# adaLN vectors as groups of 32-partition matmuls, scale1 in column blocks, one more ring slot, another order of pieces

## Chip, cores and metric

One core of a Trainium2 chip runs the whole layer. The metric is device time in microseconds of one execution; lower is better. Engines: PE (matmuls), DVE (vector engine), ACT (scalar engine), POOL (GpSimd), SP (the queue that issues most transfers).

## What is computed

One decoder layer on 256 tokens of width 1024, batch 1, all in float32:

```python
mod = silu(c) @ w_ada + b_ada                       # w_ada: 1024 x 6144
shift1, scale1, gate1, shift2, scale2, gate2 = split(mod, 6)
hn   = rms_norm(x, g_norm1) * (1 + scale1) + shift1
proj = hn @ w_in                                    # 1024 x 3592
q_m, k_m, v_m, o_m, gates, q_a, k_a, v_a = split(proj)
h_m  = rms_norm(mlstm(silu(conv(q_m, k_m)), v_m, gates)) * sigmoid(o_m)   # 4 heads x 128
h_a  = causal_attention(q_a, k_a, v_a)              # 8 heads x 64; one block of 256 keys
x    = x + gate1 * (concat(h_m, h_a) @ w_out)
hn2  = rms_norm(x, g_norm2) * (1 + scale2) + shift2
# router: top 1 of 4 groups, top 2 of its 8 experts; 32 SwiGLU experts, 1024 -> 512 -> 1024
x    = x + gate2 * sum_of_chosen_experts(hn2)
out  = rms_norm(x, g_final)
```

The weights are 246 MB, of which 201 MB belong to the 32 experts. All of them are read.

## The kernel before

**Ring.** All large tiles are slots of 8.3 KB per partition in one pool of 18 (`RING`): a slot takes one block of 1 MiB of weights, or a large intermediate (x1, xnT, the two halves of h, q/k of attention, and so on). Loads are issued on SP in program order; a load waits until a slot is free, and what stands behind it on SP waits too. After the mixer's 43 blocks (24 of w_ada, 14 of w_in, 4 of w_out, x in two halves) come 192 blocks of experts, six for each.

**Before the steps.** x is normalised (L260 to 263) and transposed into `xnT`. scale1 is summed over 1024 rows: three row blocks by full-width matmuls with `silu(c)` repeated over 128 columns (L252), the other five by DVE (`ada_kc`, L211), and both sums are turned into columns by 16 matmuls of one column each (L285). Then `h_scaled` (L373) forms h without shift1 as a high and a low half.

**The 72 steps.** `steps` (L300) holds seven chunks of 512 columns of w_in with eight steps of 128 rows each (`ga` with the gate columns, `ka`, `va`, `qm`, `km`, `vm`, `om`), then 16 steps of w_out. In each step a weight block is split into `hi`, rounded to fp32r, and `lo`, the rest (`split`, L322, three steps ahead); `hi` is a cast on ACT or on DVE (`ON_DVE_H`, 31 of 72), `lo` a subtraction on POOL or on DVE (`ON_DVE_L`, 24 of 72). `step` (L339) makes three products (high by high, high by low, low by high) on PE. The first two chunks use h without shift1; `shift_rows` and `shift_bias` (L386, L394) compute shift1 @ w on DVE and add it as a bias (`evac_k`, `bias_q`). From `va` on, `h_full` (L400) has put shift1 into h.

**Pieces.** Everything else (conv, attention, mLSTM, adaLN sums, loads, transposes) is a list of named pieces (`op`, L722). `PLAN` (L43) gives the step ahead of which each is put. PE runs in exactly this order; for the other engines the framework orders the instructions within the dependencies. An adaLN section is summed row block by row block with a multiply-add over 1024 columns on DVE (`ada_kc`), four of them scaled on ACT and added on POOL (`ON_POOL_A`); then `ada_cols` (L222) makes columns with one-column matmuls, or `ada_bcast` (L230) and `gate2_rows` (L712) a row repeated over all partitions.

**After the steps.** Residual, second norm, router logits, choice of experts, and the first gather `pair(0)` (L897 to 985). Then 32 experts one after another: `gate_up` (L1003) and `down` (L1019) are matmuls of 32 columns of weights that write groups of 32 PSUM partitions.

Of the kernel before, what the change touches and what calls it, by code (L numbers as in the profile page):

```python
# [19 lines left out]
P = 128  # L20
D = 1024
# [14 lines left out]
RING = 18  # L36
# [27 lines left out]
ON_DVE_H = {0, 1, 3, 4, 5, 7, 11, 15, 16, 22, 24, 28, 29, 30, 31, 32, 36, 37, 39, 40, 42, 44, 45, 48, 49, 51, 52, 58, 60, 68, 70}  # L64
ON_POOL_A = {(2, 1), (2, 3), (2, 7), (5, 6)}
# [3 lines left out]
def tile_hymba_layer(  # L69
# [63 lines left out]
    A.dma_start(pk[0:8, :], rows(g_norm2))
# [70 lines left out]
    AW, ACC = {}, {}  # L204

    def ada_row(sec):
        acc = ACC[sec] = gate2 if sec == 5 else wk.tile([P, D], F32, name=f"acc{sec}", tag="acc")
        G.memset(acc, 0.0)
        G.dma_start(acc[0:1, :], b_ada[0:1, sec * D:(sec + 1) * D])

    def ada_kc(sec, kc):  # L211
        w = AW[sec, kc // 2][:, kc % 2, :]
        if (sec, kc) in ON_POOL_A:
            A.activation(w, w, AF.Copy, scale=csil[:, kc:kc + 1])
            G.tensor_tensor(ACC[sec], ACC[sec], w, op=ALU.add)
        elif sec not in ACC:
# [5 lines left out]
    def ada_cols(sec, permuted):  # L222
        acc = ACC[sec]
        p = bank(f"pc{sec}", (P, KC))
        a = acc.rearrange("q (p j) -> q j p", j=KC) if permuted else acc.rearrange("q (j p) -> q j p", j=KC)
# [4 lines left out]
    def ada_bcast(acc, dst, name):  # L230
        for h in range(2):
            p = bank(f"{name}{h}")
            T.matmul(p, ones, acc[:, h * 512:(h + 1) * 512], start=True, stop=True)
            A.activation(dst[:, h * 512:(h + 1) * 512], p, AF.Copy)

    csb = wk.tile([P, KC // 2, P], F32, name="csb", tag="k2")
    V.tensor_copy(csb, csil.rearrange("p (q k) -> p q k", k=2)[:, :, 0:1].to_broadcast([P, KC // 2, P]))

    def load_x():
        for tb in range(NT):  # L240
            nc.sync.dma_start(x1[:, tb, :], x2[:, tb, :])

# [1 line left out]
    pr = [bank(f"pr{h}", tag="pj") for h in range(2)]  # L244
    row = gate2[0:1, :]
    for q in range(4):
        load_ada(1, q)
        if q == 1:
            load_x()
        if q < 3:  # L250
            for h in range(2):
                T.matmul(pr[h], csb[:, q, :], AW[1, q][:, 0, h * 512:(h + 1) * 512], start=(q == 0), stop=(q == 2))  # L252
        else:
            ada_kc(1, 2 * q)
        ada_kc(1, 2 * q + 1)
        if q == 2:
            A.activation(row[:, 0:512], pr[0][0:1, :], AF.Copy)
            A.activation(row[:, 512:1024], pr[1][0:1, :], AF.Copy)
# [23 lines left out]
    p1 = bank("pc1", (P, KC))  # L282
    for part, k in ((row, 1), (ACC[1], P)):
        for j in range(KC):
            T.matmul(p1[:, j:j + 1], part[:, j * P:(j + 1) * P], ones[0:k, 0:1], start=(k == 1 and j == 0),  # L285
                     stop=(k == P), skip_group_check=True)
    s1 = const([P, KC], "s1")
    V.tensor_tensor(s1, p1, bsc1, op=ALU.add)
    V.scalar_tensor_tensor(s1, s1, 1.0, g1c, op0=ALU.add, op1=ALU.mult)

# [1 line left out]
    # the first two chunks use h without shift1 and get shift1 @ w as a bias  # L292
# [29 lines left out]
    def split(s):  # L322
# [8 lines left out]
        (V if s in ON_DVE_L else G).tensor_tensor(lo, src, hi.bitcast(F32), op=ALU.subtract)  # L331
# [967 lines left out]
```

## Time and profile before

| | us |
|---|---|
| median of 3 runs | 692.18 |
| lowest, highest | 692.13, 694.0 |
| span of the profiled execution | 690.9 |
| first projection matmul starts | 30.32 |
| last matmul of the output projection starts | 210.42 |
| first expert matmul starts | 226.74 |

The span runs from the first to the last instruction of one profiled execution; the median is 1.3 us above it. Over the whole span PE is busy 546.9 us (79%), DVE 286.1 (41%), ACT 128.5 (19%), POOL 116.7 (17%), and 248.80 MB are moved at a mean of 360 GB/s. These shares are means over stages that differ: read the 40 slices first (busy tenths of each engine, the transfers' share, GB/s), then the table by stage, then single lines of the timeline.

### The profile page before, as it was taken

The numbers are of one execution on the slowest core, as the hardware profiler recorded it, in microseconds if no ns is written. First come the engines' busy times: TensorE is split into PE (matmuls) and PEld (weight loads), VectorE is DVE, ScalarE is ACT, GpSimd is POOL, SyncE is SP. The second block draws the span as 40 slices with busy tenths as digits, with TensorE's granted clock in tenths as the row PEclk, the third lists the DMA queues.
The fourth block names the chain that finished last, engine by engine and source line by source line (L and its number), as shares of the span: only waits on it lengthen the run. The fifth ranks groups of instructions, "written<-read, shape, count | busy, mean of one in ns | idle before, by whom it ended". The sixth has DMA issues, their size and how long they took to land. (4 is left out here: it accounts for less than half of the span.)

```text
span 690.9 us, 15508 instructions
## 1 busy us (share of the span) xinstructions
PE 546.9 (79%) x6817; PEld 405.4 (59%) x6817; DVE 286.1 (41%) x609; ACT 128.5 (19%) x286; POOL 116.7 (17%) x109
## 2 busy tenths in 40 slices
PE   3998899699899898777777767686896877787575
PEld 1798688587687775663544545374564645454353
DVE  2699999999976432212212122122212122131212
ACT  2525445358325100000000000000000000000023
POOL 4265377646630100000000000000000000000000
PEclk9698889999879999979987988977788698698788
DMA  8999926558877899999999999999999999999992
GB/s 283 397 393 372 331 67 244 182 184 313 296 305 247 355 411 415 413 420 415 416 414 419 413 416 417 415 416 416 415 415 415 416 417 416 415 414 417 413 362 105
DMA packets 52864, 248.80 MB, mean 360 GB/s; under 512 B 4229, under 2 KB 4377, under 8 KB 36409
## 3 DMA queue, kind: packets, MB, share of 16 engines
q1 hardware_dynamic: 52256, 247.52, 90.2%
q8 instruction: 55, 0.90, 0.5%
q0 software_dynamic: 368, 0.20, 0.3%
q14 instruction: 17, 0.13, 0.0%
q10 hardware_dynamic: 168, 0.06, 0.0%
HBM read 246.70 MB, written 1.05 MB: 359 GB/s over the span
## 5 line engine op out<-in xcount | busy, mean ns | idle before, releaser
L1005 PE MATMUL pgu<-we,xg 128*32 128x128 f32 x4096 | 153.1, 302 | 56.1 <-DMA we<-in_w_expert_gate_dram 26.9
L1005 PEld LDWEIGHTS pgu<-we,xg 128*32 128x32 f32 x4096 | 124.9, 122 | 95.2 <-issue 36.7
L1021 PE MATMUL py<-wd,ht 128*32 128x256 f32 x992 | 78.6, 452 | 31.1 <-DVE ht L1016 15.6
L1012 DVE TENSOR_TENSOR hm<-sg,pgu 128x128 f32<-128x128 f32 x32 | 9.2, 288 | 220.4 <-ACT sg L1010 220.4
L1026 DVE TENSOR_TENSOR y<-py,gate 32x256 f32<-32x256 f32 x124 | 52.1, 420 | 92.3 <-PE py L1021 90.9
L1010 ACT ACTIVATE sg<-pgu 128x128 f32<-128x128 f32 x32 | 8.9, 277 | 392.5 <-PE pgu L1005 388.4
L882 PEld LDWEIGHTS pgx<-oh,xn 128*128 128x128 f32 x512 | 66.4, 211 | 6.0 <-issue 6.0
L882 PE MATMUL pgx<-oh,xn 128*128 128x64 f32 x512 | 69.9, 298 | 0.0
L1021 PEld LDWEIGHTS py<-wd,ht 128*32 128x32 f32 x992 | 31.3, 123 | 63.9 <-DVE ht L1016 22.6
L220 DVE SCALAR_TENSOR_TENSOR acc<-wa,csil,acc 128x1024 f32<-128x1024 f32 x30 | 49.4, 1647 | 4.9 <-DMA wa<-in_w_ada_dram 4.5
L872 POOL TENSOR_TENSOR ow<-oh,gg 128x128 f32<-128x128 f32 x16 | 5.9, 399 | 217.5 <-PE pw L1032 183.3
L825 PE MATMUL acc<-y,owt 128*128 128x512 f32 x64 | 34.6, 667 | 1.9 <-DVE y L1026 1.9
L1195 POOL MEMSET owz<- 128x1024 f32 x1 | 1.0, 951 | 201.5 <-PE pgu L1005 201.5
L1014 PE MATMUL ph<-ident,hm 128*128 128x128 f32 x32 | 10.8, 338 | 17.0 <-DVE hm L1012 17.0
L331 POOL TENSOR_TENSOR wl<-wo,wh 128x512 fp32r<-128x512 f32 x12 | 22.2, 1866 | 10.8 <-ACT wh L330 8.5
L886 DVE TENSOR_TENSOR xg<-pgx,s 128x256 f32<-128x256 f32 x32 | 12.2, 420 | 28.1 <-PE pgx L882 27.2
L825 PEld LDWEIGHTS acc<-y,owt 128*128 128x128 f32 x64 | 11.8, 206 | 15.0 <-issue 11.4
L1014 PEld LDWEIGHTS ph<-ident,hm 128*128 128x128 f32 x32 | 5.2, 161 | 24.5 <-DVE hm L1012 24.5
L337 PE MATMUL po<-wh,hTL 128*128 128x512 f32 x32 | 13.9, 433 | 4.4 <-DVE hTL L632 4.3
L252 PE MATMUL pr<-wa,csb 128*128 128x512 f32 x12 | 9.3, 917 | 8.5 <-DMA wa<-in_w_ada_dram 8.5
L335 PE MATMUL po<-wh,hTH 128*128 128x512 f32 x32 | 14.5, 452 | 0.0
L1016 DVE COPY ht<-ph 128x128 f32<-128x128 f32 x32 | 9.2, 289 | 10.4 <-PE ph L1014 10.4
(371 smaller groups left out, 883.1 us busy)
## 6 DMA issues: line engine op xcount, KB each, us to landing
we<-in_w_expert_gate_dram SPq DMA_DIRECT2D x64, 1024.0 KB, 20.0
we<-in_w_expert_up_dram SPq DMA_DIRECT2D x64, 1024.0 KB, 20.0
wd<-in_w_expert_down_dram SPq DMA_DIRECT2D x63, 1024.0 KB, 20.3
wa<-in_w_ada_dram SPq DMA_DIRECT2D x24, 1024.0 KB, 8.2
wo<-in_w_out_dram SPq DMA_DIRECT2D x4, 1024.0 KB, 5.0
wi_ga<-in_w_in_dram SPq DMA_DIRECT2D x2, 1040.0 KB, 11.2
wi_ka<-in_w_in_dram SPq DMA_DIRECT2D x2, 1024.0 KB
wi_qm<-in_w_in_dram SPq DMA_DIRECT2D x2, 1024.0 KB, 18.3
```

The lines of the kernel that those rows point to most:

```text
L220: V.scalar_tensor_tensor(ACC[sec], w, csil[:, kc:kc + 1], ACC[sec], op0=ALU.mult, op1=ALU.add)
L252: T.matmul(pr[h], csb[:, q, :], AW[1, q][:, 0, h * 512:(h + 1) * 512], start=(q == 0), stop=(q == 2))
L331: (V if s in ON_DVE_L else G).tensor_tensor(lo, src, hi.bitcast(F32), op=ALU.subtract)
L335: T.matmul(p, aH, bH, start=first, stop=False)
L337: T.matmul(p, aL, bH, start=False, stop=last)
L825: T.matmul(acc2[tb, h][:, cols], lhsT, rhs, start=start, stop=stop, skip_group_check=True)
L882: T.matmul(pj[j], xn2[:, tb, j, :], oh(tb), start=(tb == 0), stop=(tb == NT - 1))
L886: V.tensor_tensor(xg[:, js], src, s2[:, js].unsqueeze(2).to_broadcast([P, 4, n]), op=ALU.mult)
L1005: T.matmul(pgu[32 * g:32 * g + 32, u * P:(u + 1) * P], xg[:, j, :], wt[:, g * P:(g + 1) * P], start=j == 0 and u == 0, stop=j == KC - 1, s ...
L1014: T.transpose(ph, hm, ident)
L1021: T.matmul(py[32 * g:32 * g + 32, :], ht[:, 32 * f:32 * f + 32], wt[:, g * S:(g + 1) * S], start=first, stop=last, skip_group_check=True)
L1026: V.tensor_tensor(y4[r0:r0 + 32, g * S:(g + 1) * S], py[32 * g:32 * g + 32, :], gate2[r0:r0 + 32, g * S:(g + 1) * S], op=ALU.mult)
```

## The change

- `RING` goes from 18 to 19 slots; the DMA scratch of POOL's software queue is set to 4096.
- An adaLN section is summed in one PSUM tile of 128 x 256: partitions 32g to 32g+31 hold column part g (`ada_mm`, four matmuls of 32 weight columns for each source). Eight row blocks (shift1, gate1) or six of eight (scale2, shift2, gate2) are still multiply-adds on DVE (`ada_dve`, `ON_DVE_A`), whose sum enters as one more source; POOL does none.
- Columns come out of this tile with a masked product and a reduction (`own_column`, mask `m32`) in place of one-column matmuls; gate rows with `ada_rows` and two matmuls for each half (`ada_bcast`).
- scale1 is loaded as four blocks of 1024 rows x 256 columns (`load_scale1`) and formed in four parts before steps 0, 2, 4 and 6 (`scale1`).
- shift1 @ w for the first two chunks moves from DVE to such matmuls (`shift_bias`); the gate projection becomes eight matmuls of 256 columns and two small ones (`gate_rows8`, `gate_proj`).
- x is the first large load; the small vectors are split between ACT's and POOL's queues; xn is scaled on DVE.
- All `hi` casts are on ACT; `lo` is on POOL in 30 of 72 steps and otherwise on DVE; the first operation of `h_full` moves from ACT to DVE.
- `LOADS` and `PLAN` are rewritten; the transposes of x1's first half stand between the two halves of the last step.

```diff
-RING = 18
+RING = 19
 LOADS = """
-    ga0 ga1 ka0 ka1 A00 A01 A02 A03 qm0 va0 qm1 km0 va1 om0 vm0 km1 A20 vm1 A21 A40 A22 om1 W2 A23 A41 W1 A30 A42 W0
-    W3 A43 A31 A32 A50 A51 A33 A52 A53
+    ga0 B1 B2 ga1 B3 ka0 ka1 A00 A01 A02 A03 va0 va1 qm0 A20 qm1 A21 A22 A23 km0 km1 vm0 vm1 A40 om0 A41 om1 A42 A43 W2 W3
+    A30 A31 W0 A32 W1 A33 A50 A51 A52 A53
 PLAN
...
-    ldA33:41 ldA50:40 ldA51:41 ldA52:41 ldA53:41 gw0:5 gw1:6 sh0:-3 sh1:-3 sh2:-3 sh3:0 sh4:0 sh5:0 sh6:0 sh7:1
+    scl:24 hs0:-2 hs1:-2 sb1:1 hs2:1 hs3:1 sb2:3 hs4:3 hs5:3 sb3:4 hs6:4 hs7:4 a00:7 a01:8 a02:8 a03:9 a04:9 a05:10
+    a06:10 a07:11 a24:20 a25:21 a26:22 a27:23 a44:39 a45:40 a46:41 a47:42 a34:53 a35:54 a36:55 a37:56 a54:62 a55:63
+    ldqm1:2 ldkm0:11 ldkm1:12 ldvm0:17 ldvm1:17 ldA20:-3 ldom0:18 ldom1:19 ldA21:4 ldA22:9 ldA23:10 ldA40:17 ldW2:22
+    ldW3:33 ldA41:18 ldA42:20 ldW0:41 ldW1:42 ldA43:21 ldA30:37 ldA31:40 ldA32:41 ldA33:45 ldA50:49 ldA51:51 ldA52:53
+    ldA53:53 gw0:5 gw1:6 ad0:15 shc:15 sbq:16 sbk:17 hf0:15 hf1:15 hf2:15 hf3:15 hf4:15 hf5:15 hf6:16 hf7:16 eq0:8
+    eq1:8 eq2:8 eq3:8 bq0:17 bq1:17 bq2:17 bq3:17 ek0:17 ek1:17 ek2:17 ek3:17 eva0:24 eva1:24 vm1:33 gp0:18 gp1:19
+    dec3:31 am0:19 ae0:19 ap0:22 av0:25 am1:20 ae1:20 ap1:23 av1:26 am2:21 ae2:21 ap2:24 av2:26 am3:22 ae3:22 ap3:25
+    av3:27 an3:27 am4:23 ae4:23 ap4:26 av4:29 am5:25 ae5:25 ap5:28 av5:30 am6:27 ae6:27 ap6:30 av6:31 am7:28 ae7:28
+    ap7:31 av7:32 an7:32 c0_3:32 c0_2:32 c0_1:32 c0_0:32 c1_3:32 c1_2:33 c1_1:33 c1_0:33 c2_3:33 c2_2:34 c2_1:34
+    c7_2:43 c7_1:43 c7_0:43 silu:44 evm0:48 evm1:48 mn:56 mg0:57 mg1:57 hta:32 ms0:51
+    ms1:51 ms2:52 ms3:52 mp0:54 mp1:55 ht4:36 ht5:36 ht6:38 ht7:38 ht0:61 ht1:62 ht2:63 ht3:64 row2:16 row5:60 ad2:26
+    pb1:48 ad4:50 sc2:50 ad3:58 sc3:58 ad5:64 tri:40 a20:18 a21:19 a22:20 a23:21 a40:38 a41:39 a42:40 a43:41 a30:51
...
-ON_DVE_L = {0, 2, 3, 4, 5, 6, 9, 15, 16, 22, 25, 26, 29, 33, 35, 47, 48, 50, 51, 52, 56, 61, 64, 70}
-ON_POOL_A = {(2, 1), (2, 3), (2, 7), (5, 6)}
+ON_POOL_L = {s for s in range(72) if (s % 2 if 28 <= s < 64 else s % 3 == 2)}
+ON_DVE_H = set()
+ON_DVE_A = {0: range(8), 2: range(8), 4: range(6), 3: range(6), 5: range(6)}
...
+    m32 = const([P, 32], "m32")
+    V.tensor_reduce(m32, ident.rearrange("p (g m) -> p m g", g=4), axis=AX.X, op=ALU.add)
...
+    def ada_mm(sec, kcs, first=True, last=True):
+        if first:
+            AP[sec] = bank(f"pa{sec}", (P, S))
+        srcs = [(csb[:, kc, :], AW[sec, kc // 2][:, kc % 2, :]) for kc in kcs]
+        if last and sec in ACC:
+            srcs.append((ones[:, 0:32], ACC[sec]))
+        for i, (a, b) in enumerate(srcs):
+            for g in range(4):
+                o = AP[sec][32 * g:32 * g + 32, :]
...
+                T.matmul(o, a, ada_part(sec, b, g), start=first and i == 0, stop=last and i == len(srcs) - 1)
+    def own_column(p, n, inner, dst, name):
+        t = wk.tile([P, 32 * n], F32, name=name, tag="sm", bufs=3)
+        if inner:
+            V.tensor_tensor(t.rearrange("p (j m) -> p j m", j=n), p.rearrange("p (j m) -> p j m", j=n),
+                            m32.unsqueeze(1).to_broadcast([P, n, 32]), op=ALU.mult)
+            V.tensor_reduce(dst, t.rearrange("p (j m) -> p j m", j=n), axis=AX.X, op=ALU.add)
...
+    def ada_rows(sec):
+        r = ROWS[sec] = wk.tile([P, S], F32, name=f"rows{sec}", tag="rows", bufs=1)
+        V.tensor_tensor(r, AP[sec], BG[sec], op=ALU.add)
+    def ada_bcast(sec, dst, name, h):
+        p = bank(f"{name}{h}")
+        for i in range(2):
+            g = 2 * h + i
+            T.matmul(p[:, i * S:(i + 1) * S], ident[:, 32 * g:32 * g + 1].to_broadcast([P, P]), ROWS[sec],
+                     start=i == 0, stop=True, skip_group_check=True)
+        A.activation(dst[:, h * 512:(h + 1) * 512], p, AF.Copy)
...
+    def scale1(b):
+        p = bank(f"ps1{b}", (P, 64))
+        for kc in range(KC):
+            for g in range(4):
+                T.matmul(p[32 * g:32 * g + 32, :].rearrange("p (j m) -> p j m", j=2), csb[:, kc, :],
+                         SB[b][:, kc, :].rearrange("p (j g m) -> p g j m", j=2, g=4)[:, g],
+                         start=kc == 0, stop=kc == KC - 1)
+        js = s1[:, 2 * b:2 * b + 2]
+        own_column(p, 2, True, js, f"d1{b}")
...
+    for tb in range(NT):
+        nc.sync.dma_start(x1[:, tb, :], x2[:, tb, :])
+    load_scale1(0)
...
-        (V if s in ON_DVE_L else G).tensor_tensor(lo, src, hi.bitcast(F32), op=ALU.subtract)
+        (G if s in ON_POOL_L else V).tensor_tensor(lo, src, hi.bitcast(F32), op=ALU.subtract)
...
     def shift_bias(i):
-        p = bank(f"pbs{i}", (P, 4))
-        for j in range(4):
-            T.matmul(p[:, j:j + 1], BA[i][:, j * P:(j + 1) * P], ones[:, 0:1], start=True, stop=True)
-        V.tensor_copy(pbias[:, i, :], p)
+        p = bank(f"pbs{i}", (P, P))
+        for kc in range(KC):
+            for g in range(4):
+                T.matmul(p[32 * g:32 * g + 32, :].rearrange("p (f m) -> p f m", f=4), shb[:, kc, :],
+                         w_of(ORDER[i], kc).rearrange("p (f g m) -> p g f m", f=4, g=4)[:, g],
+                         start=kc == 0, stop=kc == KC - 1)
+        own_column(p, 4, True, pbias[:, i, :], f"dbs{i}")
...
+        for kc in range(KC):
+            g = kc % 4
+            T.matmul(p[32 * g:32 * g + 32, :], wg[:, kc, :], xnT[:, kc, :], start=kc < 4, stop=kc >= 4)
...
+                    if tb == 0:
+                        for t in range(NT):
+                            x1_T(t, 0)
...
-    nc = _bacc.Bacc("TRN2", target_bir_lowering=False, num_devices=1)
+    nc = _bacc.Bacc("TRN2", target_bir_lowering=False, num_devices=1, dynamic_dma_scratch_size=4096)
```

## Rows read from the trace of the kernel before

**Rows 1.** The page's 40 slices: DVE's busy tenths, the transfers' share, GB/s

```profile
DVE  2699999999976432212212122122212122131212
...
DMA  8999926558877899999999999999999999999992
GB/s 283 397 393 372 331 67 244 182 184 313 296 305 247 355 411 415 413 420 415 416 414 419 413 416 417 415 416 416 415 415 415 416 417 416 415 414 417 413 362 105
```

**Rows 2.** Busy time by stage: stretch, length, each engine busy (instructions), clock, DMA share, GB/s

```profile
30.30:65.10 34.80, 32.02 (x224) 31.21 (x224) 32.42 (x39) 15.93 (x36) 18.08 (x10) 0.85 1.03 387
65.10:108.50 43.40, 38.68 (x217) 32.03 (x217) 40.07 (x79) 19.62 (x44) 24.35 (x18) 0.88 0.58 203
108.50:165.90 57.40, 52.18 (x325) 44.88 (x323) 53.49 (x97) 31.63 (x81) 32.98 (x28) 0.97 0.64 230
165.90:210.80 44.90, 40.48 (x166) 32.25 (x164) 37.42 (x43) 15.77 (x29) 23.23 (x13) 0.81 0.74 281
```

**Rows 3.** Timeline of PE where the experts begin: start, us, instruction, count, idle before

```profile
226.74 3.70 PE L1005 MATMUL pgu<-we,xg 128*32 128x128 f32 x128
...
231.87 1.93 PE L1021 MATMUL py<-wd,ht 128*32 128x256 f32 x32 [0.39 <-DVE ht L1016]
233.62 1.06 PE L1005 MATMUL pgu<-we,xg 128*32 128x128 f32 x32
234.61 3.79 PE L882 MATMUL pgx<-oh,xn 128*128 128x64 f32 x32
```

**Rows 4.** Busy time by stage: all up to the experts

```profile
0.00:226.70 226.70, 195.91 (x1083) 162.91 (x1083) 184.88 (x323) 104.57 (x219) 109.35 (x91) 0.89 0.77 279
```

**Rows 5.** Timeline of PE and ACT at the start

```profile
7.08 1.19 PE L252 MATMUL pr<-wa,csb 128*128 128x512 f32 x1 [3.23 <-DMA wa<-in_w_ada_dram]
...
14.02 1.06 ACT L194 ACTIVATE xn<-x 128x1024 f32<-128x1024 f32 x1 [8.97 <-DMA x<-in_x_dram]
...
19.27 1.15 ACT L263 ACTIVATE xn<-x,r 128x1024 f32<-128x1024 f32 x1 [0.23 <-DVE r L189]
```

**Rows 6.** DVE's groups by line up to 225: count, busy, mean ns, idle before

```profile
L220 DVE SCALAR_TENSOR_TENSOR acc<-wa,csil,acc 128x1024 f32<-128x1024 f32 x30 | 49.4, 1647 | 4.9 <-DMA wa<-in_w_ada_dram 4.5
...
L392 DVE SCALAR_TENSOR_TENSOR sba<-wi_ka,sh,sba 128x512 f32<-128x512 f32 x7 | 7.2, 1026 | 0.0
...
L328 DVE CAST wh<-wo 128x512 fp32r<-128x512 f32 x4 | 4.8, 1210 | 0.0
...
L612 DVE TENSOR_TENSOR hh<-hh,rh 128x512 f32<-128x512 f32 x2 | 4.5, 2278 | 0.0
...
L331 DVE TENSOR_TENSOR wl<-wi_ga,wh 128x512 fp32r<-128x512 f32 x6 | 4.1, 692 | 1.4 <-ACT wh L330 1.2
...
L651 DVE TENSOR_REDUCE cbs<-wrs 128x36 f32<-128x288 f32 x1 | 0.6, 649 | 0.0
...
L642 DVE TENSOR_TENSOR wrs<-wst,sh 128x256 f32<-128x256 f32 x1 | 0.4, 420 | 0.0
```

**Rows 7.** Timeline of DVE and, below, of POOL in the same stretch

```profile
61.98 0.74 DVE L392 SCALAR_TENSOR_TENSOR sba<-wi_ga,sh,sba 128x512 f32<-128x512 f32 x1
...
62.98 1.77 DVE L392 SCALAR_TENSOR_TENSOR sba<-wi_ka,sh,sba 128x512 f32<-128x512 f32 x1
...
62.55 6.46 POOL L331 TENSOR_TENSOR wl<-wi_va,wh 128x512 fp32r<-128x512 f32 x4 [7.39 <-ACT wh L330]
```

**Rows 8.** The adaLN sums on DVE: count, shortest/median/longest ns, first and last start

```profile
L220 DVE SCALAR_TENSOR_TENSOR acc<-wa,csil,acc x29: 1265/1286/2383, 19.2 to 191.7; 128x1024 f32<-128x1024 f32 x29
```

**Rows 9.** Timeline of PE in the output projection

```profile
175.58 0.80 PE L337 MATMUL po<-wh,hTL 128*128 128x512 f32 x1 [4.27 <-DVE hTL L632]
...
192.82 7.55 PE L227 MATMUL pc<-ones,acc 128*128 128x1 f32 x32
```

**Rows 10.** Casts of weights on ACT: count, shortest/median/longest ns

```profile
L330 ACT ACTIVATE wh<-wo x12: 617/632/663, 161.1 to 193.1; 128x512 fp32r<-128x512 f32 x12
```

**Rows 11.** Timeline of SP at the first expert load

```profile
165.70 0.34 SPq L1121 DMA_DIRECT2D we<-in_w_expert_gate_dram  x1
```

More of the change, by code (lines that the diff above doesn't have):

```diff
@@ L202, in load_ada, with ada_part, ada_dve @@
         AW[sec, q] = w
[L204 to L211, printed above, removed]
+    AW, ACC, AP, ROWS = {}, {}, {}, {}
+    csb = const([P, KC, 32], "csb")
+    V.tensor_copy(csb, csil.unsqueeze(2).to_broadcast([P, KC, 32]))
+    def ada_part(sec, t, g):
+        if sec in (0, 1):
+            return t.rearrange("p (j g m) -> p g j m", j=KC, g=4)[:, g]
+        return t[:, g * S:(g + 1) * S]
+    def ada_dve(sec, kc):
         w = AW[sec, kc // 2][:, kc % 2, :]
[L213 to L216, printed above, removed]
+        if sec not in ACC:
             acc = ACC[sec] = wk.tile([P, D], F32, name=f"acc{sec}", tag="acc")
@@ L236, in tile_hymba_layer @@
[L236 to L252, printed above, removed]
-        else:
[L254 to L258, printed above, removed]
+    def ada_mm(sec, kcs, first=True, last=True):
[7 more added lines that the diff above has]
+                o = AP[sec][32 * g:32 * g + 32, :]
+                if sec in (0, 1):
+                    o = o.rearrange("p (j m) -> p j m", j=KC)
+                T.matmul(o, a, ada_part(sec, b, g), start=first and i == 0, stop=last and i == len(srcs) - 1)
@@ L260, in tile_hymba_layer @@
+    for tb in range(NT):
+        nc.sync.dma_start(x1[:, tb, :], x2[:, tb, :])
+    load_scale1(0)
+    A.activation(ss0, csil[:, 0:1], AF.Sqrt, scale=0.0, bias=eps)
     xn = slot3("xn", NT)
@@ L281, in tile_hymba_layer @@
         A.activation(xnT[:, 2 * k2:2 * k2 + 2, :], p, AF.Copy)
[L282 to L289, printed above, removed]
+    pkt = bank("pkt", (P, 56))
+    T.transpose(pkt, pa_, ident[:56, :56])
+    A.activation(col[:, 0:56], pkt, AF.Copy)
+    scale1(0)
     LA, NB = 3, 4
@@ L505, in gate_w, with gate_rows8, gate_proj @@
     def gate_w(h):
[L506 to L509 removed]
+        G.tensor_copy(wg[:, 4 * h:4 * h + 4, 0:8], WI["ga", h][:, :, 0:8])
+    GS = {}
+    def gate_rows8():
+        p = bank("pgr", (P, S))
         for kc in range(KC):
[L511 to L512 removed]
+            g = kc % 4
+            T.matmul(p[32 * g:32 * g + 32, :], wg[:, kc, :], xnT[:, kc, :], start=kc < 4, stop=kc >= 4)
+        GS[0] = wk.tile([P, S], F32, name="gsr", tag="sm", bufs=3)
+        A.activation(GS[0], p, AF.Copy)
+    def gate_proj():
+        p = bank("pg", (P, NT, 8))
+        for tb in range(NT):
+            T.matmul(p[:, tb, :], GS[0][:, tb * P:(tb + 1) * P], m32[:, 0:8], start=True, stop=True)
+        V.tensor_tensor(gt, p, gbias.unsqueeze(1).to_broadcast([P, NT, 8]), op=ALU.add)
     def gate_logs():
@@ L704, in strict_tri @@
         G.tensor_copy(ones_b, ones)
-    CB = {}
-    def last_c():
-        CB[0] = wk.tile([P, P], F32, name="csg", tag="sm", bufs=3)
-        G.tensor_copy(CB[0], csil[:, KC - 1:KC].to_broadcast([P, P]))
-    def gate2_rows(h):
-        cs = slice(h * 512, (h + 1) * 512)
-        p = bank(f"pb2{h}")
-        T.matmul(p, CB[0], AW[5, 3][:, 1, cs], start=True, stop=False)
-        T.matmul(p, ones, ACC[5][:, cs], start=False, stop=True)
-        A.activation(gate2[:, cs], p, AF.Copy)
     ops, ops_names = [], []
@@ L805, in tile_hymba_layer @@
     op("sqt", 68, 72, "xq1", sqrt_table)
-    for tb in range(NT):
-        op(f"xT{tb}", 68, 71, f"xta xu{tb}", x1_T, tb, 0)
     F = {}
@@ L919, in tile_hymba_layer @@
         acc_init(1, 1)
-        gate2_rows(0)
+        ada_bcast(5, gate2, "pb2", 0)
         pieces(75)
```

182 lines of the change are left out of this document (88 added, 94 removed).

## The prediction, made before the changed kernel was timed

> **What bounds the kernel now.** First the page's slices of 17.3 us [rows 1]. From slice 15 to slice 38 the transfers stand at 9 tenths and 411 to 420 GB/s: the expert weights, 192 blocks of 1 MiB, stream without a break while PE works beside them. At 415 GB/s a block takes 1.0486 MB / 415 = 2.53 us. Slices 6 to 14 move only 67 to 355 GB/s, while DVE shows 9 tenths from slice 3 to slice 11. So in the first third the transfers wait for the mixer, not the reverse: the ring of blocks is full, and a block comes free only when a step of the mixer is done with it.
>
> The table by stage [rows 2] says which engine holds the mixer. In the 180.5 us from the first projection (30.3) to the end of the output projection (210.8) DVE is busy 32.42 + 40.07 + 53.49 + 37.42 = 163.4 us and PE 32.02 + 38.68 + 52.18 + 40.48 = 163.4 us, 91% each; ACT 82.9 us, POOL 98.6. PE and DVE pace each other, and part of PE's share is low clock (means 0.81 to 0.97).
>
> The experts begin at 226.7 [rows 3]. From there the end is a matter of transfers: until then the core has moved 279 GB/s x 226.7 us = 63.2 MB = 60.3 blocks [rows 4]; 43 of them belong to the mixer (24 adaLN, 14 w_in, 4 w_out, x), so some 17 expert blocks are in, a ring of 18 less one. The other 175 x 2.53 = 443 us lead to 670, in slice 39, where the rate falls off. So **the end moves one for one with the moment at which the experts begin**, as long as the ring is full by then, down to the floor for that moment at which the transfers never pause: (43 + 18) x 2.53 + 4 = 158 us.
>
> **Part 1, the start.** Today w_ada's blocks stand ahead of x and around it in SP's queue; the first is in at 7.1, and x reaches ACT only at 14.0 [rows 5]. RMS, scaling and transposes, the full-width matmuls and the one-column sums lead to the first projection at 30.3. The change loads x (1 MiB) first, so I set its landing at 6.5, then one block that holds two of the eight scale columns. ACT's chain from x to the end of xn took 14.0 to 20.4, 6.4 us [rows 5]; a table load in it gets an earlier place, and half the scaling goes beside it on DVE, so 5. Transposes, copies, the scale block's matmuls and its sums add 6 to 7. The first projection then starts at 18 (bounds: 15, if these overlap better; 22, if the 7 us from the start to a first landing repeat for the second block). Gain 12 us.
>
> **Part 2, DVE's work in the 72 steps.** What goes, in today's busy time, one row standing for each kind [rows 6]: the 16 shift-bias operations, 14.4 us; of 31 casts of weights (`hi`, 20.7 us in eight rows) the 28 in this window, 19.6; of the adaLN sums (36 in two rows, 49.4 + 9.1 us) 53.3, with three first terms 55.5; the 24 differences (`lo`, eight rows), 20.7 us. Left over are 163.4 - 110.2 = 53.2 us. Some 15 of them I count as stretching (the two row scalings at 2278 ns are three times a 512-column operation [rows 6]), so 38 us undisturbed.
>
> What comes, undisturbed: adaLN sums of 34 row blocks, 29 x 1.27 [rows 8] and 5 first terms at 0.75 (by the rows 755 ns each), 40.6; 42 differences x 0.69 = 29.0 [rows 6]; eight h scalings moved from ACT, at the router's 256-column product 8 x 0.42 = 3.4 [rows 6]; nine column extractions, each a masked product and a reduction of 64 to 256 columns, by the router's 0.42 and 0.65 us [rows 6] at most 1.07 and together some 6.4; small adds 1.6. Sum 81, and with the 38 left 119 us.
>
> To that comes stretching. A two-input operation of 0.74 us takes 1.77 us while POOL runs its differences [rows 7], and an adaLN sum between 1.27 and 2.38 [rows 8]. I count 40 us of it on DVE (adaLN 13, the kinds that stay 15, casts and differences 9, shift bias 3), beside 98.6 us of POOL [rows 2]. POOL goes from 48 differences to 30 and loses its four adaLN sums: about 46 us, so 40 x 46 / 98.6 = 19 us. DVE: **138 us** instead of 163 (bounds: 119 without stretching, 159 with all of today's).
>
> **Part 3, PE's work.** Gone: one-column sums, 7.55 us for the 32 just ahead of the last step [rows 9] and 3.2 for 16 earlier ones, shift-bias columns 2.7, gate projections 3.7, together 17.1. New are matmuls into 32 partitions. The experts show their price: 128 of 128 columns in 3.70 us and 32 in 1.06, so 0.029 to 0.033 us; 32 of 256 columns in 1.93, 0.06 at most [rows 3]. Three scale blocks 96 x 0.033 = 3.2, two shift biases 64 x 0.033 = 2.1, 44 sums x 0.055 = 2.4, gate rows 0.9, together 8.6. No row shows 64 columns in this form, so the scale blocks lie between half the 128-column price and all of it; I take all, the difference is 1.6 us. 163.4 - 17.1 + 8.6 = 155 at today's clock. At full clock throughout, each stage's busy time times its mean clock [rows 2], 163.4 would be 145 and the result some 140.
>
> Weighed against this: no gap shows where a 32-partition group gives way to a full-width one (the group at 233.62 ends at 234.68, the next starts at 234.61 [rows 3]), so the rows price that change at nothing. The Trainium skill, "TensorEngine Tiling (Array Packing)", section Tiling Modes, says that changing the tiling mode drains the engine. Twelve such groups mean 24 changes; at an estimated 0.28 us, a short matmul's duration here, the sum would be 6.7 us later. I go by the rows.
>
> **Part 4, wall time of the steps.** At today's 91%, DVE's 138 us make 152 us and PE's 140 to 155 make 154 to 170. I take 158 us instead of 180.5. Inside it lies the chain behind the mLSTM norm, on which PE waits 4.27 us [rows 9]; the change starts it two steps earlier, I let it stay. All 72 casts on ACT: 31 x 0.63 [rows 10] = 19.5 more, less 4.1 (h scalings) and 4.6 (weights scaled for POOL): 93.8 of 158 us. Cover enough; where ACT waits, its casts are queued behind, and PE has three steps in hand.
>
> **Part 5, router and ring.** From 210.8 to 226.7 the chain stays; of two gate2 matmul groups ahead of the gather half the columns go, -0.9: 15 us. The 19th slot lets one more block land before the experts: -2.5 us (0, if a slot is not free in time). A53, behind which all experts queue on SP, moves from step 41 to 53. Today slots, not the step, hold it: the first expert load goes out at 165.7 [rows 11], 61 us ahead of the experts, for 17 x 2.53 = 43 us of transfers. Step 53 falls at about 18 + 53 x 2.2 = 134; 57 us remain and 18 blocks need 45.5, covered by 11 us. POOL's smaller DMA ring serves the small vectors and is costed at nothing: they have over 10 us before a step needs them.
>
> **Sum.** Steps end at 18 + 158 = 176, experts begin at 191, 35.7 us earlier; with the slot 38.2. Span 690.9 - 38.2 = 652.7. The median of the runs is 692.18, 1.3 above the span, so **654 us**.
>
> **Rivals.** (1) DVE stays the pace: POOL's differences stretch as much as today. For it: from step 16 to 31 the plan puts a second section of sums and all eight score heads. 159 / 0.91 = 175 us of steps, experts at 208, 671 us. Against it: POOL has half the work. (2) PE runs nearly unbroken at full clock: 140 us of steps from 16 on, experts at 171, above the floor of 158; 634 us. Against it: no stage today holds both full clock and full share. (3) The loads do not follow: expert blocks find slots only from about step 62 (154), 37 us before the experts, 14.6 blocks instead of 18; 663 us, and 672 at twice that shortage. Then the change does not do what it says, the 19th slot included. (4) Slower: ACT as the only maker of `hi`. It is one in-order queue, and each wait on DVE's maxima or on PE's transposes holds the casts behind it and so PE. It decides from 195 us of steps on, 2.71 us a step against today's 2.51; ACT would need 101 us of waits beside its 94 of work, while today it stands idle 97.6 us in all. At 200 us of steps the experts begin at 233, 6.3 later, less the slot: 696 us.
>
> **How the numbers follow.** Forecast 0.50, (1) 0.21, (2) 0.16, (3) 0.08, (4) 0.05. The range 634 to 673 reaches from rival 2 to rivals 1 and 3; outside are (4) and what lies past the two ends. About 0.3% (2 us) is what a measurement of this kernel tells from no change; faster 0.94, same 0.01, slower 0.05.
>
> **What would show it.** First projection near 18; DVE's busy time from there to the end of the output projection near 138, in about 158; no one-column sums before the last step; experts near 191, about 18 of their blocks moved by then, transfers near 415 GB/s from then on. It is wrong if the experts begin late in spite of a smaller DVE sum (then what PE waits on is the answer), or if transfers pause after they begin.

## The result, and the profile after

| | us |
|---|---|
| before, median of 4 runs | 693.04 |
| after, median of 4 runs (lowest, highest) | 668.9 (668.35, 670.15) |
| ratio of after to before, 95% interval | 0.9662 (0.9641 to 0.9684) |
| forecast, and its range | 654.0 (634 to 673) |
| profiled execution after: time, span | 668.35, 666.6 |
| first projection starts, output projection ends, first expert matmul | 19.96, 187.6, 203.9 |

The kernel is 24 us faster; the forecast was 38. The range holds the time, but the likeliest value is 15 us off.

The slices of the page (16.7 us each; DVE's busy tenths, the transfers' share, GB/s) answer to [rows 1]:

```profile
DVE  2589878978764323112131212121211213122112
...
DMA  9999963789977999999999999999999999999982
GB/s 269 378 396 399 394 267 98 281 275 392 414 249 296 417 413 414 416 416 415 419 415 415 416 416 418 413 416 415 417 416 416 415 416 415 417 417 415 414 335 94
```

The dip of the transfers still lies in the mixer, and from slice 14 on they stream at 413 to 419 GB/s. The table by stage answers to [rows 2]: stretch, length, then PE, weight loads, DVE, ACT and POOL busy (instructions), clock, DMA share, GB/s. The stretches are `ga`, `ka`, `va`, `qm`, `km`, `vm`, `om`, the output projection, the router, and all steps:

```profile
20.00:40.00 20.00, 17.47 (x289) 15.91 (x290) 11.82 (x29) 7.68 (x16) 2.77 (x3) 0.91 1.05 391
40.00:57.30 17.30, 14.22 (x171) 13.26 (x169) 16.69 (x23) 7.92 (x18) 5.74 (x3) 1.00 1.04 394
57.30:82.00 24.70, 23.00 (x173) 15.51 (x169) 22.43 (x53) 15.98 (x38) 4.98 (x4) 1.00 1.04 396
82.00:106.80 24.80, 24.80 (x190) 21.70 (x190) 19.18 (x54) 14.68 (x42) 9.08 (x15) 1.00 0.52 200
106.80:120.20 13.40, 12.90 (x108) 12.57 (x108) 13.36 (x24) 8.73 (x18) 6.95 (x6) 1.00 0.67 225
120.20:137.30 17.10, 14.60 (x57) 11.61 (x57) 15.95 (x24) 7.88 (x15) 7.22 (x5) 0.90 0.71 251
137.30:155.50 18.20, 18.20 (x114) 14.85 (x113) 14.20 (x19) 11.65 (x34) 6.25 (x4) 1.00 0.86 309
155.50:187.60 32.10, 29.30 (x171) 21.49 (x170) 23.06 (x40) 16.55 (x32) 8.24 (x6) 1.00 0.95 384
187.60:203.90 16.30, 16.30 (x105) 12.67 (x104) 10.27 (x47) 9.58 (x12) 0.00 (x0) 0.90 0.74 259
...
20.00:187.60 167.60, 154.49 (x1257) 126.89 (x1258) 136.68 (x259) 91.06 (x204) 51.23 (x44) 0.98 0.86 326
```

DVE's busy time in the steps is 136.7 us, as forecast (138), yet the steps took 167.6, not 158. DVE's share is uneven: 96, 100 and 93% in `ka`, `km` and `vm`, but 59% in `ga`, 77 in `qm`, 78 in `om` and 72 in the output projection. PE reads 92% over all steps, at a clock of 0.98. By this table PE holds the steps, and that was my first theory. The runs below speak against it.

### The profile page after: what moved, and what is told of

It is laid out like the page before. It is cut to its first block, busy times and chain, and to the rows that moved or that the text cites. A ratio compares the mean times of both kernels' runs of the same rounds, so it can differ in the third digit from the quotient of the medians.

```text
span 666.6 us, 16232 instructions
## 1 busy us (share of the span) xinstructions
PE 525.3 (79%) x7174; PEld 390.7 (59%) x7174; DVE 254.2 (38%) x609; ACT 138.1 (21%) x305; POOL 70.2 (11%) x91
## 5 line engine op out<-in xcount | busy, mean ns | idle before, releaser
L1060 PE MATMUL py<-wd,ht 128*32 128x256 f32 x992 | 74.9, 433 | 30.2 <-DVE ht L1055 16.6
L921 PE MATMUL pgx<-oh,xn 128*128 128x64 f32 x512 | 75.7, 314 | 0.0
L921 PEld LDWEIGHTS pgx<-oh,xn 128*128 128x128 f32 x512 | 72.1, 226 | 5.9 <-issue 5.7
L1060 PEld LDWEIGHTS py<-wd,ht 128*32 128x32 f32 x992 | 29.8, 119 | 59.9 <-DVE ht L1055 21.5
L226 DVE SCALAR_TENSOR_TENSOR acc<-wa,csil,acc 128x1024 f32<-128x1024 f32 x29 | 42.7, 1471 | 0.1
L1053 PE MATMUL ph<-ident,hm 128*128 128x128 f32 x32 | 10.4, 325 | 17.5 <-DVE hm L1051 17.5
L1053 PEld LDWEIGHTS ph<-ident,hm 128*128 128x128 f32 x32 | 4.9, 154 | 24.8 <-DVE hm L1051 24.8
L373 PE MATMUL po<-wl,hTH 128*128 128x512 f32 x32 | 12.7, 398 | 0.7 <-DVE wl L368 0.7
L367 ACT ACTIVATE wh<-wo 128x512 fp32r<-128x512 f32 x16 | 10.0, 630 | 12.4 <-PE po L374 9.4
```

The costliest lines, as they stand in the source:

```text
L367: A.activation(hi, src, AF.Copy)
L373: T.matmul(p, aH, bL, start=False, stop=False)
L921: T.matmul(pj[j], xn2[:, tb, j, :], oh(tb), start=(tb == 0), stop=(tb == NT - 1))
L1053: T.transpose(ph, hm, ident)
L1060: T.matmul(py[32 * g:32 * g + 32, :], ht[:, 32 * f:32 * f + 32], wt[:, g * S:(g + 1) * S], start=first, stop=last, skip_group_check=True)
```

## The experiments

The theories: **A**, PE holds the steps now; **B**, DVE holds them, with its stretching beside POOL; **C**, both in turn. Four runs changed one thing each in the program (diffs here and below are cut to the lines that matter):

```diff
# ring18
-RING = 19
+RING = 18
# pe_less: steps 16 to 55
-        T.matmul(p, aL, bH, start=False, stop=last)          # va, vm, om
+        if not two: T.matmul(p, aL, bH, start=False, stop=last)
+                    if i == 1 and s >= 16: continue          # qm, km
# dve_less: 29 sums on half of the columns
-            V.scalar_tensor_tensor(ACC[sec], w, csil[:, kc:kc + 1], ACC[sec], ...)
+            V.scalar_tensor_tensor(ACC[sec][:, 0:512], w[:, 0:512], csil[:, kc:kc + 1], ACC[sec][:, 0:512], ...)
# csil_first: ACT's order at the start fixed
+    with tc.manual_schedule(engines={mybir.EngineType.Activation}):
+        A.activation(csil, ckt, AF.Silu)
+        A.activation(ss0, csil[:, 0:1], AF.Sqrt, scale=0.0, bias=eps)
+        for tb in range(NT): ...                              # squares and scales of x
```

**ring18.** 

> The changed kernel with RING = 18. If the 19th slot lets one more expert block land before the experts begin, the time is one block longer, 2.5 us: 671.4 against 668.9, with the first expert matmul unmoved at about 204. If a slot is not free in time, no difference (668.9).

Measured: 692.47 (ratio to before 1.0017, 0.9994 to 1.004). Neither case: all of the gain is gone. A row of DVE's timeline and one of PE's:

```profile
34.87 0.76 DVE L224 TENSOR_SCALAR acc<-wa,csil 128x1024 f32<-128x1024 f32 x1 [14.24 <-DMA wa<-in_w_ada_dram]
...
37.59 0.58 PE L404 MATMUL pga<-hL,wh 128*128 128x256 f32 x1 [18.39 <-DVE hL L415]
```

The framework gave DVE another order: the first adaLN term now stands ahead of `hL`, waits 14.2 us for its block, and PE waits 18.4 us behind it. So the time tells nothing of the slot. The trace does count one block fewer when the experts begin: 60.6 (277 GB/s x 229.4 us) against 61.4 in after. And the run tells much of the method: an edit here also re-orders the engines that have no order of their own in the kernel.

**pe_less.** 

> The changed kernel without one of the three products in steps 16 to 55 (low by high in va, vm and om, high by low in qm and km): 64 matmuls of 256 columns at a pace of 0.118 us and 48 of 512 at 0.235 us, 18.8 us less work for PE; DVE, ACT, POOL and the loads keep all of theirs. Theory A (PE holds the steps after the change): 650 to 655. Theory B (DVE, stretched by POOL, and the chains between engines hold them, and PE is only busy beside): 664 or more.

Measured: 669.47 (0.960 to 0.972 of before). Theory A fails here; B's range holds.

**dve_less.** 

> The changed kernel with the 29 adaLN multiply-adds on DVE over 512 of 1024 columns (half of each sum is left out): about 29 x 0.6 = 17 us less for DVE, or more where they were stretched; PE, ACT, POOL and the loads unchanged. Theory A (PE holds): 665 to 669. Theory B (DVE holds): 650 to 657.

Measured: 662.31 (0.9556 to 0.9612 of before): less than B asks, far more than A allows. In both runs DVE's and ACT's orders had moved too (as they did in csil_first and, later, in f_best), so both were repeated with the order held.

**csil_first.** 

> The changed kernel with ACT's order fixed at the start: Silu and the first Sqrt before the two squares, so that two of four table loads of 1.28 us go and two stand before x lands. The second row block's scale is ready some 3 us earlier, the first projection starts at about 17 instead of 19.96. If the start goes to the end one for one: 666. If the first chunk is then held by its second weight block, which lands at about 24 and cannot come earlier: 667.5 to 669.

Measured: 668.82, no gain beside after (0.9672 of before for 0.9662). The first projection starts at 17.9 and the first expert matmul at 202.9 (203.9 in after): in the profiled execution one of 2.1 us was left when the experts began. ACT at the start, first after, then csil_first:

```profile
4.51 1.06 ACT L200 ACTIVATE xn<-x 128x1024 f32<-128x1024 f32 x1 [1.10 <-DMA x<-in_x_dram]
...
5.67 1.28 ACT L194 ACT_TABLE_LOAD   x1
...
7.28 1.28 ACT L189 ACT_TABLE_LOAD   x1
8.58 0.18 ACT L189 ACTIVATE csil<-ckt 128x8 f32<-128x8 f32 x1
...
9.81 1.28 ACT L297 ACT_TABLE_LOAD   x1
```

```profile
4.08 1.28 ACT L298 ACT_TABLE_LOAD   x1
...
15.25 2.19 ACT L368 ACTIVATE wh<-wi_ga 128x512 fp32r<-128x512 f32 x4 [2.43 <-DMA wi_ga<-in_w_in_dram]
17.34 0.89 ACT L415 ACTIVATE hH<-xnT,s 128x256 fp32r<-128x256 f32 x2
```

In after, Silu stands between the two square roots and costs two extra table loads. Without them ACT waits for the first weight block of `ga`, and `hH` is queued behind four casts: the start meets the next limit at 17.3. It is the first weight block, not the second as I had expected.

**The order held.** In the next kernels each instruction of DVE, ACT and POOL up to the experts is tied, by dependencies that order without waiting, to its place in after (`tc.add_manual_dep` with a NoSync edge between neighbours). The traces show DVE's instructions in the order of after. One part of the program then changes alone.

**h_after.** 

> The changed kernel itself once more, as the measure for the runs beside it: every instruction of DVE, ACT and POOL up to the experts is tied by order-only dependencies to the place that it has in the changed kernel, so the program is the same: 668.9, within 0.2%.

Measured: 672.06 (669.25 to 673.02; 0.9718 of before), 3 us above after, on another chip, and outside the 0.2% that I expected: the measure for this group. Its profile was taken at 669.25 us, those of h_slot18 and h_mix2 below at 676.54 and 673.7, so these traces lie further apart than the medians.

**h_pe_less.** 

> The run pe_less again (one of three products left out in steps 16 to 55, 18.8 us less work for PE), but with DVE's, ACT's and POOL's instructions held in the order of the changed kernel, so that PE's work alone differs. Theory A (PE holds the steps): 650 to 655. Theory B (DVE, stretched by POOL, and the chains between engines hold them): 664 or more. Theory C (they hold by turns, stage by stage): 656 to 663.

Measured: 671.24. **h_dve_less.** 

> The run dve_less again (29 adaLN multiply-adds over half of their columns, some 17 us less work for DVE, 25 with the stretching that goes with it), with DVE's, ACT's and POOL's instructions held in the order of the changed kernel. Theory A (PE holds): 665 to 669. Theory B (DVE holds): 645 to 655. Theory C (by turns): 656 to 664.

Measured: 661.31. The steps as a whole, in h_after, h_pe_less and h_dve_less (columns as in the table by stage):

```profile
20.50:188.60 168.10, 156.95 (x1257) 129.36 (x1258) 136.82 (x259) 90.68 (x204) 51.40 (x44) 0.97 0.86 323
```

```profile
20.20:188.90 168.70, 148.53 (x1145) 119.92 (x1146) 137.22 (x259) 89.93 (x204) 50.51 (x44) 0.90 0.86 323
```

```profile
19.90:180.20 160.30, 153.15 (x1257) 127.13 (x1258) 117.22 (x259) 91.36 (x204) 45.05 (x44) 0.98 0.89 341
```

18.8 us less work for PE leave the length of the steps as it was. PE's busy time falls by 8.4 us alone, as the granted clock falls from 0.97 to 0.90: a busy share of 92% did not show a bound. 19.6 us less busy time on DVE shorten the steps by 7.8 and the run by 10.8 (8.5 between the two profiled executions). By the ranges on record the first run falls into B's and the second into C's: DVE's time counts, but less than one for one comes back.

**h_slot18.** 

> The changed kernel in its own order, with one ring slot taken out of use behind the last mixer load until expert 16, so that the mixer has 19 slots and the experts begin with 18. If the 19th slot is worth one block of transfers at the moment the experts begin: 671.4 (2.5 more than the changed kernel), first expert matmul unmoved. If the ring is not full by then: 668.9.

```diff
+        if t == "A53":
+            SPARE[0] = slot("spare")
+            nc.sync.dma_start(SPARE[0][:, 0:16], x2[:, 0, 0:16])
...
+        if e == 16:
+            G.tensor_tensor(SPARE[0][:, 1:2], SPARE[0][:, 0:1], ht[:, 0:1], op=ALU.add)
```

Measured: 673.54 (0.9712 to 0.9758) against 672.06 (0.9695 to 0.9741): 1.5 us, with intervals that overlap. In the profiled execution 60.6 blocks were moved when the experts began (304 GB/s x 209.03 us) against 61.5 in h_after (315 x 204.83): the slot holds one block, as forecast. From there to the end it took 465.8 us against 462.7, but h_both took 465.1 with 19 slots and before 464.2 with 18, so what the block is worth in time stays open. The first expert matmul came 4.2 us later; the table of stages below leads to the reason.

**Three more in the held order:**

```diff
# h_both: pe_less and dve_less together
# h_pool_less
-        (G if s in ON_POOL_L else V).tensor_tensor(lo, src, hi.bitcast(F32), op=ALU.subtract)
+        if s in ON_POOL_L:
+            G.tensor_tensor(lo[:, 0:64], src[:, 0:64], hi[:, 0:64].bitcast(F32), op=ALU.subtract)
+            WS[s] = hi, hi
+            return
+        V.tensor_tensor(lo, src, hi.bitcast(F32), op=ALU.subtract)
# h_mix2
-ON_DVE_A = {0: range(8), 2: range(8), 4: range(6), 3: range(6), 5: range(6)}
+ON_DVE_A = {0: range(4), 2: range(6), 4: range(4), 3: range(6), 5: range(6)}
-    ad4:50 sc2:50
+    ad4:46 sc2:47
```

**h_both.** 

> The two cuts of h_pe_less and h_dve_less in one kernel, in the held order (one product of three left out in steps 16 to 55, half of the columns of 29 adaLN sums left out). Measured apart they gave 0.8 and 10.8 us against the changed kernel (672.06 on that chip). If DVE and PE hold by turns, stage by stage, the two together give more than their sum, since each cut uncovers the other: 643 to 654. If DVE alone holds, PE's cut is again worth nothing: 659 to 662.

Measured: 663.5, above both ranges (0.9596 of before; h_dve_less 0.9574). C fails as I had put it: at the end PE's cut is worth nothing here either. The trace says where it goes: the output projection begins at 144.0 (148.0 in h_dve_less), its last matmul starts at 176.2 (179.8), and the router takes 2.7 of these 3.6 us back. PE ahead of the experts, h_dve_less and then h_both:

```profile
192.69 3.75 PE L922 MATMUL pgx<-oh,xn 128*128 128x64 f32 x32
...
196.42 3.70 PE L1045 MATMUL pgu<-we,xg 128*32 128x128 f32 x128
```

```profile
189.09 6.44 PE L925 MATMUL pgx<-oh,xn 128*128 128x64 f32 x32
...
195.51 5.87 PE L1048 MATMUL pgu<-we,xg 128*32 128x128 f32 x128
```

The same matmuls take 2.7 and 2.2 us longer at the lower clock (0.83 from 178.2 to 195.5; 1.00 in the router of h_dve_less). The 0.9 us that are left at the first expert matmul do not reach the end either. h_mix2 shows the same `pgx` (6.29).

**h_pool_less.** 

> The changed kernel in its own order with POOL's 30 differences cut to 64 of 512 columns; in these steps the second product takes the high half in place of the low one, so the output leaves out their low parts, and PE has the same work. DVE keeps its own work and loses only its stretching beside POOL, which the prediction put at 19 us. If that stretching lies where DVE holds the steps: DVE busy about 120 to 124 in place of 138, and 657 to 664. If it lies where PE holds, or if DVE is not stretched by POOL: 668 or more.

Measured: 657.3 (0.9477 to 0.9535), the largest gain of all, with DVE's work untouched. Its steps, and DVE's sums in `ka` (in after 3.62 and 3.48 for two):

```profile
19.00:175.80 156.80, 152.31 (x1257) 127.21 (x1258) 120.71 (x259) 91.74 (x204) 22.93 (x45) 0.98 0.92 349
...
43.71 2.60 DVE L226 SCALAR_TENSOR_TENSOR acc<-wa,csil,acc 128x1024 f32<-128x1024 f32 x2
```

DVE falls from 136.8 to 120.7 us: 16.1 us of stretching by 30 differences, 0.54 us each, and the steps shrink from 168.1 to 156.8. On DVE itself such a difference takes 0.69 us: putting it on POOL frees DVE of 0.15 us only, on average. PE's waits for DVE in the steps add up to 10.4 us in h_after (11.5 in after), 6.5 in h_dve_less and 4.0 here. For POOL itself PE waited 0.2 us in h_after, so POOL's own lateness is not what went. The two longest of these waits, in after:

```profile
PE pvm L372 <- DVE cvb L601: 3.0, 2, 2.5
PE pa L239 <- DVE acc L226: 2.9, 1, 2.9
```

The figures are the total in us, how often, and the longest.

**h_mix2.** 

> The changed kernel, order held, with 8 more of the adaLN row blocks on PE: four of shift1, two of gate1, two of scale2, whose multiply-adds on DVE lie in the stages where DVE is busy 90 to 100% (ka, va, km, vm). DVE loses 8 x 1.47 = 11.8 us, PE gets 8 x 0.43 = 3.4 us. By turns: 661 to 667, faster than the changed kernel. If PE holds everywhere: 674 to 676.

Measured: 668.99 (0.9665 of before, 0.9634 to 0.9696), beside 0.9718 (0.9695 to 0.9741) for h_after: between the two ranges. It is not slower, so PE does not hold everywhere, and at most a little faster. `om` began 2.7 us earlier (135.5 for 138.2); `om` itself and the router gave that back (experts at 207.8). The size of the gain stays open.

**f_best.** 

> What the runs so far point to, put together in a complete kernel: Silu and the first Sqrt ahead of the squares (as in csil_first), ten more adaLN row blocks on PE (four of shift1, two each of gate1, scale2, shift2), and nine of POOL's 30 differences on DVE, those of ka, of vm and of the last steps, beside which DVE is stretched. DVE -10 x 1.47 + 9 x 0.69 = -8.5 us and less stretching, PE +4.3, POOL -14. The order of DVE, ACT and POOL is left to the framework. If DVE and its stretching hold the steps: 657 to 664, by the start about -2, ka -4, vm -3, the last stage -1 to -3 against the changed kernel's 669 to 672. If PE holds, or takes the gain back at a lower clock: 666 to 674.

```diff
# csil_first, and
-ON_POOL_L = {s for s in range(72) if (s % 2 if 28 <= s < 64 else s % 3 == 2)}
+ON_POOL_L = {s for s in range(72) if (s % 2 if 28 <= s < 64 else s % 3 == 2)} - {8, 11, 14, 41, 43, 45, 47, 68, 71}
-ON_DVE_A = {0: range(8), 2: range(8), 4: range(6), 3: range(6), 5: range(6)}
+ON_DVE_A = {0: range(4), 2: range(6), 4: range(4), 3: range(4), 5: range(6)}
-    ad4:50 sc2:50
+    ad4:46 sc2:47
```

Measured: 658.65 (657.91 to 659.14), 0.952 of before (0.9498 to 0.9542), with the whole of the computation: 10 us below after.

```profile
18.40:178.40 160.00, 156.92 (x1337) 129.87 (x1338) 122.15 (x257) 90.71 (x204) 36.40 (x37) 0.98 0.91 344
```

DVE has 14.5 us less, PE 2.4 us more than after, and the steps are 7.6 us shorter. When the stages begin, read from PE's rows of each chunk:

| | ga | ka | va | qm | km | vm | om | out | experts |
|---|---|---|---|---|---|---|---|---|---|
| after | 20.0 | 40.0 | 57.3 | 82.0 | 106.8 | 120.2 | 137.3 | 155.5 | 203.9 |
| h_after | 20.5 | 40.7 | 60.4 | 83.0 | 107.8 | 121.2 | 138.2 | 156.4 | 204.8 |
| h_pe_less | 20.2 | 40.4 | 60.1 | 83.5 | 106.6 | 119.4 | 133.3 | 156.4 | 205.5 |
| h_dve_less | 19.9 | 40.6 | 55.4 | 78.5 | 103.2 | 116.0 | 129.8 | 148.0 | 196.4 |
| h_pool_less | 19.0 | 39.0 | 54.1 | 77.2 | 101.9 | 114.6 | 128.6 | 146.8 | 192.0 |
| f_best | 18.4 | 38.1 | 54.0 | 77.5 | 103.1 | 115.8 | 131.0 | 147.6 | 194.6 |

Read down: what DVE is spared shows in `ka` (about 17 to 20 us long, 15 to 16 when DVE is relieved) and again in `vm` (17, then 14 to 15). PE's cut shows too: `vm` takes 13.9 us in h_pe_less, and `qm`, which keeps its 24 to 26 us in every row where PE's work is whole, takes 23.1.

h_pe_less is 4.9 us ahead at `om` and level with h_after when the output projection begins. Its `om` takes 23.1 us for 18.2: the clock fell to 0.85, and PE waited 2.1 us for ACT and 2.3 for `st` of DVE. In h_after it waited for neither. Ahead of `st` two tiny DVE operations now fall behind POOL's differences. The first of them in h_after, then in h_pe_less with POOL's difference and PE's wait:

```profile
147.03 0.16 DVE L691 TENSOR_TENSOR s<-s,colp 128x8 f32<-128x8 f32 x1
```

```profile
144.26 1.67 POOL L368 TENSOR_TENSOR wl<-wi_om,wh 128x512 fp32r<-128x512 f32 x1 [1.74 <-ACT wh L367]
144.72 1.24 DVE L694 TENSOR_TENSOR s<-s,colp 128x8 f32<-128x8 f32 x1
...
150.35 0.49 PE L637 MATMUL pn<-vv,st 128*128 128x129 f32 x2 [2.32 <-DVE st L627]
```

The same pair takes 1.26 and 1.22 us in h_slot18 and h_mix2, with the same wait of 2.3 us, and their `om` takes 23.6 us (137.0 to 160.6) and 21.4 (135.5 to 156.9): here lies part of the time that they lost. So h_pe_less alone is not a clean test of PE: part of what PE won was lost to stretching that fell elsewhere. h_both, where the pair takes 0.15 us each, limits what that can hide: of 18.8 us, 4.0 at the output projection and nothing at the end.

## Why the prediction was right, and where it was off

The forecast gain of 38.2 us and the 24.3 of the span differ by 13.9: 2.0 at the start (19.96 for 18), 9.6 in the steps (167.6 for 158), 1.3 in the router (16.3 for 15, at a clock of 0.90) and 1.0 in the slot (from the first expert matmul to the end 462.7 us, 464.2 before: 1.5 for 2.5, though kernels with 19 slots spread from 462.3 to 465.1 in this stretch).

**Experts' start moves the end: right.** From the first expert matmul to the end the seven held kernels and f_best take 462.3 to 465.8 us, wherever the experts begin between 192 and 209. The first projection after, and the first expert matmul, which answers to [rows 3]:

```profile
19.96 0.38 PE L404 MATMUL pga<-hH,wh 128*128 128x256 f32 x1 [2.37 <-ACT hH L414]
...
203.89 3.70 PE L1044 MATMUL pgu<-we,xg 128*32 128x128 f32 x128
```

**Part 1: right in kind.** x reached ACT at 4.5, 2 us earlier than I set it, and ACT's table loads took that and more. I had counted on one load in an earlier place; Silu made it four. In csil_first 2 us at the start left one at the experts and none in the medians, so the mistake is not shown to cost the end anything.

**Part 2: right.** 136.7 for 138; undisturbed 120.7 (h_pool_less, still with POOL's short differences) for 119; stretching 16.1 for 19. DVE and POOL in after, the pattern that answers to [rows 7] and [rows 8]:

```profile
45.16 3.62 DVE L226 SCALAR_TENSOR_TENSOR acc<-wa,csil,acc 128x1024 f32<-128x1024 f32 x2
48.70 0.69 DVE L368 TENSOR_TENSOR wl<-wi_ka,wh 128x512 fp32r<-128x512 f32 x1
49.31 3.48 DVE L226 SCALAR_TENSOR_TENSOR acc<-wa,csil,acc 128x1024 f32<-128x1024 f32 x2
```

```profile
45.08 1.31 POOL L368 TENSOR_TENSOR wl<-wi_ka,wh 128x512 fp32r<-128x512 f32 x1 [2.19 <-ACT wh L367]
49.35 2.36 POOL L368 TENSOR_TENSOR wl<-wi_va,wh 128x512 fp32r<-128x512 f32 x1 [2.96 <-ACT wh L367]
```

Two sums take 2.60 us where POOL's difference has 64 columns (h_pool_less), 1.27 each undisturbed. Beside a POOL difference of 512 columns that began 0.08 us before them they take 3.62; where DVE began 0.04 us first, POOL's difference took 2.36 in place of 1.31 and the two sums 3.48. The Trainium skill, "SBUF — State Buffer", section "SBUF: two separate sides", says that a DVE operation with two SBUF inputs and a POOL operation that reads SBUF take a shared port pair for a whole instruction, whichever starts first. By that the first pair would take 1.23 + 2.55 = 3.8 us and the second 1.27 + 1.1 + 1.27 = 3.6: the trace agrees to 0.2.

**Part 3: a term mis-sized, without effect.** PE's 154.5 us lie at the upper bound (155), but by luck: with the term as it measured, the sum at the old clock would be 162, and the clock rose from 0.81 to 0.97 by stage to 0.98. The 8.6 us for the new matmuls measured 15.3: 32-partition sums 6.3 (forecast 2.4), shift biases 4.0 (2.1), scale blocks 3.4 (3.2), gate rows and columns 1.6 (0.9). The error is one of units: the trace keeps two records for each float32 matmul of the program (an expert's 64 `gate_up` matmuls are the x128 of [rows 3]), and I multiplied the time of a record by a number of matmuls:

```profile
L431 PE MATMUL pbs<-wi_ga,shb 128*32 128x128 f32 x64 | 2.0, 274 | 0.2 <-PE pka L404 0.2
```

That is 32 matmuls of 128 columns, 0.061 us each. h_pe_less and h_mix2 show that some us of PE, either way, do not move the end. On the change of tiling the rows nearly held. PE in `ga` around a scale block, then in `om` behind a full-width float32 group:

```profile
31.91 0.28 PE L404 MATMUL pga<-hH,wl 128*128 128x256 f32 x1
32.12 1.10 PE L286 MATMUL ps<-wb,csb 128*32 128x64 f32 x64
33.15 0.39 PE L404 MATMUL pga<-hH,wh 128*128 128x256 f32 x1
33.37 0.28 PE L404 MATMUL pga<-hL,wh 128*128 128x256 f32 x1
33.49 0.28 PE L404 MATMUL pga<-hH,wl 128*128 128x256 f32 x1
...
144.34 0.38 PE L623 MATMUL sp<-cvb 128*128 128x128 f32 x2
144.48 0.48 PE L372 MATMUL pom<-wh,hH 128*128 128x512 f32 x1
144.80 0.39 PE L373 MATMUL pom<-wl,hH 128*128 128x512 f32 x1
145.03 0.39 PE L374 MATMUL pom<-wh,hL 128*128 128x512 f32 x1
```

The matmul ahead of the group starts 0.21 us before it, and the first two full-width matmuls after it are 0.22 us apart; the next are 0.12. That is 0.1 us at each end, 2.4 us for 12 groups at most, and the second 0.1 us is no price of the tiling: behind the full-width group the first two are 0.32 us apart and the next 0.23. The Trainium skill, "TensorEngine Tiling (Array Packing)", section Tiling Modes, has the engine drained at each change; the 6.7 us estimated from it are not there.

**Part 4: the step that failed.** "At today's 91%, DVE's 138 us make 152 us and PE's 140 to 155 make 154 to 170. I take 158 us instead of 180.5." DVE's share fell to 82%. The 91% of before was itself a mean over stages of 92 to 93% and one of 83 [rows 2]; the change took DVE's work out unevenly, and where DVE is light now (`ga`, `qm`, `om`, the output projection) PE's work or a wait sets the length: `qm` takes 24.8 us, all of them PE's. The larger of the two busy times, summed over the eight stages, is 158.8 us, and 8.8 us of waits come on top; the 158 had no term for them. Most of PE's waits in the steps are for DVE, and h_pool_less, where they fall from 10.4 to 4.0 us, does the steps in 156.8. PE's 154.5 us at 92% give the measured 167.6 as well, but that agreement is no cause: h_pe_less has PE at 148.5 us and takes 168.7. Of the other items, the wait behind the mLSTM norm, which I let stay, is gone, and ACT is busy 91.1 us (93.8 forecast).

**Part 5: right.** SP's first expert load went out at 147.5, 56 us ahead, and 61.4 blocks were moved at 203.9 (316 GB/s x 203.9), 18.4 of them experts'.

**The rivals.** (1) had the mechanism, DVE with its stretching, and nearly the time (671), though not its premise: DVE was at 136.7 us, not 159. (2) had the clock (0.98), but neither PE's 140 us nor its share came. (3): the loads followed. (4): PE waited 3.6 us on ACT in all of the steps. The time lies in the range and near rival (1) partly by luck: with the forecast DVE sum, at a share that nobody forecast.

## What to carry to other kernels

Sum each stage by its own larger engine and add a term for the waits between engines; a share over several stages is no price. The sum of stages alone (158.8) would have missed these 167.6 us as the forecast did. Before you trust a busy share of 90%, take an eighth of that engine's work away: if the end stays, look in the trace for what it waits on, and for where the time won was given back. And hold the order of the engines when one part is to be tested alone: a change of one pool size cost some 24 us through an order that nobody wrote.

## Not expected of the hardware

- A two-input subtraction of 128x512 on POOL (1.27 to 1.31 us alone) costs DVE 0.54 us of stretching on average; on DVE it would take 0.69 us. A DVE operation of 8 columns took 1.24 us for 0.16 when it fell behind one.
- With 18.8 us of its work removed, PE was granted 0.90 in place of 0.97 over the steps, and its busy time fell by 8.4 us only; in h_both gains of PE in the steps were lost again to matmuls at the lower clock (6.44 for 3.75 us) in the router.
- The same instructions in the same order on two chips differed by 3 us (668.9, 672.06; 0.9662 and 0.9718 of before on each).
